# Choosing experts: a second top 16 over 72 sums, a 16-bit key lookup, and another share of weight splits between two engines

## The chip, the core and the metric

The kernel runs on one core of one Trainium2 chip. The metric is the device time of one execution, in microseconds (us). The engines are TensorE (PE in the profile, with its weight loads as PEld), VectorE (DVE), ScalarE (ACT), GpSimd (POOL) and SyncE (SP, which issues the weight loads from memory here).

## What is computed

The reference is a network of two blocks over 256 tokens of 1024 features: a block with two mixers and a layer of 16,384 experts, and two layers of a second kind. Only the experts' layer matters here. Each of 8 heads forms two queries of 128 features for a token and scores them against 128 sub keys each. The 16 best of either side give 256 sums, the 16 best sums name 16 experts, and their scores become softmax weights.

```python
def peer(h, w_pq, sub_keys, expert_u, expert_v):
    ...
        q = (xb @ w_pq).reshape(PEER_BLOCK, PEER_HEADS, 2, PEER_DKH)
        s = jnp.einsum('thpd,hpkd->thpk', q, sub_keys).astype(jnp.float32)
        sv, si = lax.top_k(s, PEER_TOPK)
        cand = (sv[:, :, 0, :, None] + sv[:, :, 1, None, :]).reshape(PEER_BLOCK, PEER_HEADS, -1)
        cidx = (si[:, :, 0, :, None] * N_KEYS + si[:, :, 1, None, :]).reshape(PEER_BLOCK, PEER_HEADS, -1)
        best, pos = lax.top_k(cand, PEER_TOPK)
        eidx = jnp.take_along_axis(cidx, pos, axis=-1)
        g = jax.nn.softmax(best, axis=-1)
        act = jax.nn.gelu(jnp.einsum('thkd,td->thk', expert_u[eidx], xb).astype(jnp.float32), approximate=False)
        return jnp.einsum('thk,thkd->td', (g * act).astype(xb.dtype), expert_v[eidx])
```

## The kernel before

The kernel does not gather experts. It computes the first product for all 16,384 of them on PE (`A = gelu(U x)`), multiplies in the weight with which a token picked an expert (0 for the rest), and multiplies by V. Products keep full precision by three passes (`mm3`, L272 to L274): a weight piece of 128x1024 is loaded (`raw`), its upper part `wh` is made by ACT (L287), its lower part `wl = raw - wh` by DVE or POOL (`split_into`, L291; the argument `lo` names the engine), and PE multiplies upper by upper (L272), lower by upper and upper by lower (L273, L274). One such piece against 256 tokens is a *tile*: 24 matmuls, 3 for each of 8 groups of 128 features.

In `peer` the stage of interest runs two generators in turn (`lanes`, one step of each). `first()` makes the first 36 (`NJ1`) of 128 tiles of U; `up(j, lo)` is one. `second()` makes the choice: for each of 16 pairs of head and side (`hp`) a tile of the query weight `w_pq`, ACT's copy `pq` of the result, matmuls against the sub keys (`skey`), and for each of two token blocks a `top16` over 128 scores: `max`, `max_index`, `match_replace`, `max`, `max_index`, all on DVE. A `yield` in `second()` lets one tile of U follow. The parts `wh` and `wl` of the stage lie in four buffers each (`self.spool = tp, 4`), raw pieces in six.

`choose` is advanced by `second()` with `next(ch)`. For each head and block it makes the 256 sums `cand` (L1034) and their `top16` into `best` and `pos`. After every second head it looks up keys for 64 picks at once (two heads, two blocks, 16 picks): the position is cut into two digits (`dig`, L1043, L1044; `digf`, L1046), each digit is compared with 0 to 15 (`eq`, L1052), the hits are multiplied by the key numbers `sif` (L1056) and reduced over the 16 (`ijw`, L1058). At the end come the softmax and, behind the last tile of U (`issue_after`), six transposes on PE (L1076), whose result `IJ` and `W2` ACT copies. Everything behind waits for them: the next stage builds one-hot rows (`oo`, L939, on DVE; `ow`, L941, on POOL) and goes through the other 92 tiles of U.

Ahead of the stage stands `join`: the end of a norm over the tokens' features, for block 0 and then block 1. Its inverse root is nine operations of one column on DVE (`rsqrt`, L400 to L408, named `rq`), after which ACT makes a diagonal `jdg`, PE transposes, and DVE makes the lower parts of the features.

Each engine works through its instructions in a fixed order, which a scheduling layer has made from the program's order and dependencies. An instruction that waits holds up all behind it on its engine.

Of the kernel before, what the change touches and what calls it, by code (L numbers as in the profile page):

```python
# [38 lines left out]
NE = 1  # L39
LOS = 4  # L40
# [17 lines left out]
# ---------------------------------------------------------------- constants of the shapes  # L58
def consts():
# [71 lines left out]
    # how many of the three dilated windows hold the key, as 8 * log  # L131
# [14 lines left out]
def _fm2(w, cols):  # L146
    """256 columns as two halves of _fm, one behind the other."""
    return np.concatenate([_fm(w, cols[:P]).reshape(P, -1), _fm(w, cols[P:]).reshape(P, -1)], 1)


def _fm(w, cols):
    """[1024, n] columns -> [128, 8, n]: row k*128+p on partition p."""
    w = np.asarray(w)[:, cols]
    return np.ascontiguousarray(w.reshape(-1, P, w.shape[1]).transpose(1, 0, 2))


def _col(v):
    """[m*128] -> [128, m]."""
# [86 lines left out]
class Split:  # L245
    """An operand as the sum of two parts that a float32r pass carries exactly."""
# [11 lines left out]
class Kern:  # L258
# [7 lines left out]
    # ------------------------------------------------------------ small helpers  # L266
# [30 lines left out]
    def raw(self, src, i=0, k=1, n=1024):  # L297
        """Piece i of n columns of src, as k rows."""
# [10 lines left out]
    def wsplit(self, src, n=1024, **kw):  # L309
        """Parts of a piece of a weight that lies in SBUF."""  # L310
# [6 lines left out]
    def wtail(self, src):  # L317
        """Parts of a piece of a weight [P, 1024], each half on its own."""
# [6 lines left out]
    def finish(self, acc, parts):  # L325
        """The last terms of a sum in four banks (token block, half of the features): first those of block 0."""
# [10 lines left out]
    def stack(self, pieces):  # L337
        """Parts of pieces [P, KD, 128] of a weight, side by side."""
# [7 lines left out]
    def stacked(self, ws, hT, b, toks):  # L346
        """Features of a token block, tokens on partitions: steps for the products and for the way out of PSUM."""
# [8 lines left out]
    def rowmm(self, sums, hT, b):  # L356
        """Sums over the features of a token block, tokens on partitions; the lower parts of the features last."""
# [9 lines left out]
    def unstack(self, toks, out):  # L367
        """out[:, i * T + t] = the features i * 128 .. of token t, from both token blocks."""
# [4 lines left out]
    def warm(self, n):  # L373
        """Keeps the clock of the tensor engine up while it has nothing to do."""
# [15 lines left out]
    def cols_of(self, out, r):  # L390
        """The same for rows that lie in SBUF."""
# [4 lines left out]
    def rsqrt(self, a):  # L396
        """1/sqrt of a few columns: a first guess r from the bits, then r * p(a r^2), p in two quadratic factors."""
# [13 lines left out]
    def rsqrt_cols(self, src, n, scale):  # L411
        """1/sqrt(scale * src + EPS)."""
# [4 lines left out]
    def bcast_row(self, out, col, start=True):  # L417
        """out[p, t] = col[t] for 128 tokens."""
# [10 lines left out]
    def S(self, shape, dt=F32, name="t"):  # L429
        """A tile from the slots of its size class; a slot is free again after the last use of its tile."""  # L430
# [13 lines left out]
    # ------------------------------------------------------------ the program  # L444
# [31 lines left out]
    # ------------------------------------------------------------ block 1 up to the experts  # L476
    def block1(self):
# [20 lines left out]
        # norm1: statistics per token  # L498
# [15 lines left out]
        def modulate(c):  # L514
            """Shift and scale of 128 features; the sum over the rows of the weight in two parts."""
# [20 lines left out]
        def feature(c):  # L536
            """128 features of the tokens on partitions: context tokens, then latent ones."""
# [15 lines left out]
        def latents(c):  # L553
            """What these features add to the latents of MLA."""
# [1442 lines left out]
```

## Time and profile before

| | |
|---|---|
| time, median of 3 runs | 1949.08 us (1948.21 to 1951.96) |
| span of the profiled execution | 1946.6 us |
| PE busy | 1861.9 us, 96% |
| DVE busy | 1343.9 us, 69% |
| ACT busy | 970.3 us, 50% |
| POOL busy | 370.0 us, 19% |
| PE's share of the chain that ended last | 80% |
| DVE's share of it | 14% |

The profile is of one execution on the chip, whose time is its span and some 2.5 us around it by the median of the runs. The busy shares are means over stages that differ. The stage in question begins at about 283 us, where PE takes up the tile `hp = 0`, and ends at about 470 us with the transposes of the choice.

### The profile page before, as it was taken

The page shows a single profiled execution, that of the slowest core. Times are in us where ns is not written, and L with a number is a line of the kernel's source. Part 1 is how long each engine was busy: PE and PEld are TensorE (multiplying, and loading weights), DVE is VectorE, ACT ScalarE, POOL GpSimd, SP SyncE. Part 2 cuts the span into 40 slices and gives each one's busy share as a digit, 9 for nine tenths or more (in the row PEclk, how much of TensorE's full clock was granted, in tenths as well). Part 3 has the DMA queues.
Part 4 walks back from the last instruction along what each step waited for, and adds up shares of the span by engine and source line. Part 5 has one row for each costly group of instructions (what it writes and reads, how often), then busy time and mean ns, then how long its engine had stood idle before and what let it go on. Part 6 is the DMA issues. An engine that isn't in the chain of part 4 may idle for free.

```text
span 1946.6 us, 32774 instructions
## 1 busy us (share of the span) xinstructions
PE 1861.9 (96%) x12634; PEld 1653.5 (85%) x12634; DVE 1343.9 (69%) x2820; ACT 970.3 (50%) x1792; POOL 370.0 (19%) x263
## 2 busy tenths in 40 slices
PE   7999988899999999999999999998999999989998
PEld 6775578889999999988888879987999899879997
DVE  4536669988678888655555565577788655767785
ACT  4435443334444444544444556445666564456563
POOL 0000024445554444000000002330100023300000
PEclk9999999899999999999999999999999999999999
DMA  8732544443444444655655672412567334225671
GB/s 307 242 108 87 181 135 138 145 149 125 150 141 141 142 141 143 211 188 187 191 185 184 195 246 92 137 66 87 170 220 239 120 98 131 66 87 163 195 231 62
DMA packets 85101, 302.93 MB, mean 156 GB/s; under 512 B 10096, under 2 KB 10992, under 8 KB 84816
## 3 DMA queue, kind: packets, MB, share of 16 engines
q1 hardware_dynamic: 84944, 300.83, 47.4%
q8 instruction: 99, 1.62, 0.4%
q14 instruction: 58, 0.48, 0.1%
HBM read 298.56 MB, written 2.10 MB: 154 GB/s over the span
## 4 chain that ended last, share of the span: by engine, by line
PE 80%; DVE 14%; ACT 3%; DMA 1%; issue 1%; SPq 0%; POOLq 0%; DVEq 0%; POOL 0%; ACTq 0%
PE b L274 21%; PE b L272 20%; PE b L273 20%; PE b L277 15%; DVE wl L291 3%; DVE eq L1056 1%; DVE oo L939 1%; PE b L1122 1%; PE b L522 1%; DMA raw<-in_wv 1%; PE b L1313 1%; ACT wh L287 1%; DVE eq L1052 0%; DVE cand L1034 0%; ACT jj L722 0%
## 5 line engine op out<-in xcount | busy, mean ns | idle before, releaser
L287 ACT ACTIVATE wh<-raw 128x1024 fp32r<-128x1024 f32 x457 | 483.8, 1061 | 575.0 <-PE b L273 265.2
L291 DVE TENSOR_TENSOR wl<-raw,wh 128x1024 fp32r<-128x1024 f32 x398 | 533.6, 1341 | 264.5 <-ACT wh L287 264.1
L274 PE MATMUL b<-r,wl 128*128 128x256 f32 (+1 forms) x1216 | 350.2, 288 | 26.3 <-DVE wl L291 26.3
L272 PE MATMUL b<-r,wh 128*128 128x256 f32 (+1 forms) x1216 | 353.7, 291 | 0.0
L273 PE MATMUL b<-r,wh 128*128 128x256 f32 x1152 | 325.2, 282 | 0.0
L291 POOL TENSOR_TENSOR wl<-raw,wh 128x1024 fp32r<-128x1024 f32 x59 | 147.2, 2498 | 919.9 <-ACT wh L287 919.8
L272 PE MATMUL b<-hh,wh 128*128 128x256 f32 x1056 | 301.6, 286 | 1.7 <-DVE ast L1638 1.7
L274 PE MATMUL b<-hh,wl 128*128 128x256 f32 x1056 | 299.6, 284 | 1.8 <-DVE wl L291 1.7
L273 PE MATMUL b<-hl,wh 128*128 128x256 f32 x1056 | 298.6, 283 | 0.0
L274 PEld LDWEIGHTS b<-r,wl 128*128 128x128 f32 x1216 | 233.2, 192 | 35.0 <-DVE wl L291 33.4
L272 PEld LDWEIGHTS b<-r,wh 128*128 128x128 f32 x1216 | 234.0, 193 | 3.2 <-issue 1.5
L273 PEld LDWEIGHTS b<-r,wh 128*128 128x128 f32 x1152 | 220.9, 192 | 0.0
L272 PEld LDWEIGHTS b<-hh,wh 128*128 128x128 f32 x1056 | 202.2, 192 | 4.4 <-DVE ast L1638 2.2
L274 PEld LDWEIGHTS b<-hh,wl 128*128 128x128 f32 x1056 | 202.2, 191 | 3.1 <-DVE wl L291 3.0
L273 PEld LDWEIGHTS b<-hl,wh 128*128 128x128 f32 x1056 | 202.3, 192 | 1.4
L273 PE MATMUL b<-wl,k 128*128 128x512 f32 x492 | 194.9, 396 | 1.2 <-DVE wl L291 1.2
L272 PE MATMUL b<-wh,k 128*128 128x512 f32 x492 | 194.7, 396 | 0.0
L274 PE MATMUL b<-wh,k 128*128 128x512 f32 x492 | 194.6, 396 | 0.0
L941 POOL TENSOR_TENSOR ow<-oo,W 128x512 f16<-128x512 f16 x128 | 152.1, 1209 | 161.4 <-DVE oo L939 78.6
L1945 POOL TENSOR_TENSOR u<-u 128x256 f32<-128x256 f32 x44 | 33.5, 762 | 460.0 <-DVE u L1942 297.9
L273 PEld LDWEIGHTS b<-wl,k 128*128 128x128 f32 x492 | 92.4, 188 | 24.7 <-DVE wl L291 2.5
L274 PEld LDWEIGHTS b<-wh,k 128*128 128x128 f32 x492 | 92.4, 188 | 22.3
(480 smaller groups left out, 3189.6 us busy)
## 6 DMA issues: line engine op xcount, KB each, us to landing
raw<-in_eu SPq DMA_DIRECT2D x128, 512.0 KB, 3.9
raw<-in_ev SPq DMA_DIRECT2D x128, 512.0 KB, 3.5
raw<-in_fi SPq DMA_DIRECT2D x88, 512.0 KB, 4.6
raw<-in_w_ada SPq DMA_DIRECT2D x48, 512.0 KB, 5.5
raw<-in_wi SPq DMA_DIRECT2D x48, 512.0 KB, 3.9
raw<-in_fo SPq DMA_DIRECT2D x44, 512.0 KB, 4.6
raw<-in_w SPq DMA_DIRECT2D x16, 512.0 KB, 6.8
raw<-in_w_pq SPq DMA_DIRECT2D x16, 512.0 KB, 4.2
```

The lines of the kernel that those rows point to most:

```text
L272: mm(out, L.hi, R.hi, start=start, stop=False, skip_group_check=True)
L273: mm(out, L.hi, R.lo, start=False, stop=False, skip_group_check=True)
L274: self.lastmm = mm(out, L.lo, R.hi, start=False, stop=stop, skip_group_check=True)
L277: self.nc.tensor.matmul(out, l, r, start=start, stop=stop, skip_group_check=True)
L287: nc.scalar.activation(dst.hi, src, AF.Copy)
L291: e.tensor_tensor(dst.lo, src, dst.hi.bitcast(F32), op=OP.subtract)
L522: nc.tensor.matmul(pa[32 * j:32 * j + 32, :P], self.s2[:, 4 * h + k], wa[:, k, m * P:(m + 1) * P], start=(k == 0), stop=(k == 3), tile_pos ...
L939: nc.vector.tensor_tensor(oo[:, i], iota, IJ[:, i, None, ts].to_broadcast(B), op=OP.is_equal)
L941: nc.gpsimd.tensor_tensor(ow[:, h], oo[:, 1], W2[:, h, None, ts].to_broadcast(B), op=OP.mult)
L1056: nc.vector.tensor_tensor(e4, e4, sif[:, i, p, :, None, :].to_broadcast([P, 2, TOPK, TOPK]), op=OP.mult)
L1122: nc.tensor.matmul(pa[32 * j:32 * j + 32], self.s2[:, k], wa[:, j % 2 * 512:(j % 2 + 1) * 512], start=(k == 0), stop=(k == KD - 1), tile_p ...
L1945: nc.gpsimd.tensor_tensor(u[:, 0], u[:, 0], u[:, 1], op=OP.mult)
```

## The change

Four things change in `peer` and `choose`; a few comments and texts fall away, which shifts line numbers.

- The second top 16 looks at 72 of the 256 sums. With both lists of 16 in falling order, the sum of place a and place b can be among the 16 best only if (a + 1)(b + 1) is at most 16. Four rectangles cover these pairs: a of 0 to 1 with 16 places b, 2 to 3 with 8, 4 to 7 with 4, 8 to 15 with 1. `SV` and `SI` are laid out anew, so that both token blocks of a head are summed by one operation for each rectangle.
- The position in the 72 is turned into (a, b) by a chain of small operations on 64 columns. The lookup works on 16-bit numbers: one comparison and one multiply over 2 x 16 x 64 columns, three halving sums, and four small sums into `ijw`.
- A lookup is now two steps of `choose` (positions, then lookup), and `second()` has a `yield` ahead of every `next(ch)`, so that one tile of U stands between any two steps.
- POOL makes the lower part `wl` of 4 tiles of the query weight (`POOLQ`) and 15 of U (`POOLU`): 19 of the stage's 51, where it made 35. DVE makes the others.

```diff
+POOLQ = 3, 7, 11, 15
+POOLU = 2, 4, 6, 9, 11, 13, 16, 18, 20, 23, 25, 27, 30, 32, 34
...
-                pa = up(j, "dve" if j % 4 == 3 else "pool")
+                pa = up(j, "pool" if j in POOLU else "dve")
...
-        SV = tp.tile([P, 16, 2, TOPK], F32, name="SV")
-        SI = tp.tile([P, 16, 2, TOPK], U32, name="SI")
+        SV = tp.tile([P, 2, 2 * PH, TOPK], F32, name="SV")
+        SI = tp.tile([P, 2, 2 * PH, TOPK], U32, name="SI")
...
-                    w = self.wsplit(self.raw(I["w_pq"][hp // 2], hp % 2, KD), lo="pool" if hp % 2 else "dve")
+                    w = self.wsplit(self.raw(I["w_pq"][hp // 2], hp % 2, KD), lo="pool" if hp in POOLQ else "dve")
...
                 if hp % 2:
+                    yield
+                    next(ch)
+                if hp % 4 == 3:
+                    yield
                     next(ch)
                     yield
-                if hp % 4 == 3:
                     next(ch)
-                    yield
             next(ch)
...
+        io32 = tp.tile([P, TOPK, n], F16, name="io32")
...
+        nc.vector.tensor_copy(io32, io16[:, :, None].to_broadcast([P, TOPK, n]))
...
+        for a0, a1, w in ((0, 2, 16), (2, 4, 8), (4, 8, 4), (8, 16, 1)):
+            stairs.append((a0, a1, w, o))
+            o += (a1 - a0) * w
...
         for h in range(PH):
+            cand = tp.tile([P, 2, o], F32, tag="cand", name="cand", bufs=2)
+            hb = slice(2 * h, 2 * h + 2)
+            for a0, a1, w, at in stairs:
+                B = [P, 2, a1 - a0, w]
+                v.tensor_tensor(cand[:, :, at:at + (a1 - a0) * w].rearrange("p b (a c) -> p b a c", c=w),
+                                SV[:, 0, hb, a0:a1, None].to_broadcast(B),
+                                SV[:, 1, hb, None, 0:w].to_broadcast(B), op=OP.add)
             for b in range(2):
-                B = [P, TOPK, TOPK]
-                cand = tp.tile(B, F32, tag="cand", name="cand", bufs=2)
-                nc.vector.tensor_tensor(cand, SV[:, 2 * h, b, :, None].to_broadcast(B),
-                                        SV[:, 2 * h + 1, b, None, :].to_broadcast(B), op=OP.add)
-                self.top16(tp, cand.rearrange("p a b -> p (a b)"), best[:, h, b], pos[:, h, b])
+                self.top16(tp, cand[:, b], best[:, 2 * h + b], pos[:, 2 * h + b])
             yield
...
-            for p in range(2):
-                B = [P, n, TOPK]
-                eq = tp.tile(B, F32, tag="eq", name="eq", bufs=2)
-                nc.vector.tensor_tensor(eq, digf[:, p, :, None].to_broadcast(B),
-                                        io16[:, None, :].to_broadcast(B), op=OP.is_equal)
...
+            v.tensor_copy(p0.rearrange("p (k g) -> p g k", g=4), pos[:, hs])
+            sh = T2("sh", U32, 3)
+            for i, by in enumerate((4, 3, 2)):
+                v.tensor_scalar(sh[:, i], p0, by, None, op0=OP.logical_shift_right)
+            t, ab = T2("t", F32, 4), T2("ab", F16, 2)
+            v.scalar_tensor_tensor(t[:, 0], sh[:, 1], -2.0, sh[:, 0], op0=OP.add, op1=OP.max)
+            v.scalar_tensor_tensor(t[:, 1], sh[:, 2], -8.0, t[:, 0], op0=OP.add, op1=OP.max)
+            v.scalar_tensor_tensor(t[:, 0], p0, -56.0, t[:, 1], op0=OP.add, op1=OP.max)
...
+            eq = tp.tile([P, 2, TOPK, n], F16, tag="eq", name="eq", bufs=1)
+            B = [P, 2, TOPK, n]
+            v.tensor_tensor(eq, ab[:, :, None, :].to_broadcast(B), io32[:, None].to_broadcast(B), op=OP.is_equal)
+            e4 = eq.rearrange("p q c (k g) -> p (q c) k g", g=4)
+            v.tensor_tensor(e4, e4, sif[:, :, None, :].to_broadcast([P, 2 * TOPK, TOPK, 4]), op=OP.mult)
+            for m in (8, 4, 2):
+                v.tensor_tensor(eq[:, :, 0:m], eq[:, :, 0:m], eq[:, :, m:2 * m], op=OP.add)
+            for q in range(2):
+                e2 = eq[:, q, 0:2].rearrange("p c (k h b) -> p c k h b", h=2, b=2)
+                for b in range(2):
+                    v.tensor_tensor(ijw[:, q, b, h - 1:h + 1].rearrange("p h k -> p k h"), e2[:, 0, :, :, b],
+                                    e2[:, 1, :, :, b], op=OP.add)
+            yield
```

The order on DVE at the end of the norm ahead of the stage, before (`rq` are the nine small operations, `h` and `r` belong to the features of block 0, `iota` serves the next stage):

```order
L400 TENSOR_SCALAR rq<-jtt 128x1
L780 TENSOR_SCALAR h_2559<-b,a_2423,mod_1601 128x128
L401 TENSOR_SCALAR rq<-rq 128x1
L850 CAST iota<-io_2620 128x512
L402 TENSOR_TENSOR rq<-rq 128x1
L403 TENSOR_SCALAR rq<-rq 128x1
L781 TENSOR_TENSOR r<-h_2559,r 128x128
L404 TENSOR_TENSOR rq<-rq,jtt 128x1
L405 SCALAR_TENSOR_TENSOR rq<-rq 128x1
```

The same place after the change, from the fourth of the small operations:

```order
L405 TENSOR_SCALAR rq<-rq 128x1
L783 TENSOR_TENSOR r<-h_2559,r 128x128
L406 TENSOR_TENSOR rq<-rq,jtt 128x1
L293 TENSOR_TENSOR wl<-raw,wh 128x1024
L407 SCALAR_TENSOR_TENSOR rq<-rq 128x1
L408 SCALAR_TENSOR_TENSOR rq<-rq 128x1
L293 TENSOR_TENSOR wl<-raw,wh 128x1024
L409 SCALAR_TENSOR_TENSOR rq<-rq 128x1
L293 TENSOR_TENSOR wl<-raw,wh 128x1024
L410 SCALAR_TENSOR_TENSOR rq<-rq 128x1
L1036 CAST io_2821<-io_2822 128x1024
```

Three splits that were POOL's, and the copy that makes `io32`, now stand in DVE's queue between and behind the small operations.

The order on DVE at the first lookup (heads 0 and 1), before:

```order
L1043 TENSOR_SCALAR dig<-pos 128x64
L1044 TENSOR_SCALAR dig<-pos 128x64
L1046 CAST digf<-dig 128x128
L1052 TENSOR_TENSOR eq<-digf,io_2789 128x1024 x2
L1056 TENSOR_TENSOR eq<-eq,sif 128x512 x3
L1058 TENSOR_REDUCE ijw<-eq 128x2x2x16
L1056 TENSOR_TENSOR eq<-eq,sif 128x512
L1015 MAX SV<-b 128x8
L1058 TENSOR_REDUCE ijw<-eq 128x2x2x16
```

The same place after, from the last of the small operations on 64 columns:

```order
L1077 TENSOR_TENSOR t<-t 128x64
L1078 SCALAR_TENSOR_TENSOR ab<-p_3086,t 128x64
L1085 TENSOR_TENSOR eq<-ab,io_2821 128x2048
L1087 TENSOR_TENSOR eq<-eq,sif 128x2048
L293 TENSOR_TENSOR wl<-raw,wh 128x1024
L1089 TENSOR_TENSOR eq<-eq 128x2x512
L1089 TENSOR_TENSOR eq<-eq 128x2x256
L1089 TENSOR_TENSOR eq<-eq 128x2x128
L1020 MAX SV<-b 128x8
L1093 TENSOR_TENSOR ijw<-eq 128x16x2 x4
```

The reductions are gone, sums of two operands stand in their place, and a split has come between the parts of the lookup.

The order on DVE at the end of the stage, before (`ex` and `sm` belong to the softmax; the last two splits are the next stage's):

```order
L1058 TENSOR_REDUCE ijw<-eq 128x2x2x16
L1069 RECIPROCAL rc<-sm 128x16
L291 TENSOR_TENSOR wl<-raw,wh 128x1024
L1071 TENSOR_TENSOR ijw<-ex,rc 128x128 x2
L291 TENSOR_TENSOR wl<-raw,wh 128x1024 x2
```

After:

```order
L1089 TENSOR_TENSOR eq<-eq 128x2x512
L293 TENSOR_TENSOR wl<-raw,wh 128x1024
L1089 TENSOR_TENSOR eq<-eq 128x2x256
L1089 TENSOR_TENSOR eq<-eq 128x2x128
L1093 TENSOR_TENSOR ijw<-eq 128x16x2 x4
L944 TENSOR_TENSOR oo<-iota,IJ 128x512 x2
```

The next stage's two splits now come ahead of the last `ijw` (one is shown, the other stands a lookup earlier), and nothing but the next stage's `oo` behind it.

## Rows read from the trace of the kernel before

**Rows 1.** The page: span of the profiled execution.
```profile
span 1946.6 us, 32774 instructions
```
**Rows 2.** Busy time by stretch: us, each engine's busy us (instructions), PEclk, DMA share, GB/s.
```profile
280.00:472.00 192.00, 168.69 (x1347) 167.88 (x1348) 170.60 (x491) 75.28 (x119) 80.56 (x32) 0.91 0.42 137
300.00:320.00 20.00, 20.00 (x173) 20.00 (x172) 18.21 (x67) 9.17 (x14) 11.91 (x5) 1.00 0.47 153
342.00:344.00 2.00, 2.00 (x11) 2.00 (x11) 2.00 (x9) 0.94 (x1) 0.00 (x0) 0.50 0.29 117
```
**Rows 3.** Waits, 284 to 472 us: who for whom, us in total, times, longest.
```profile
PE b L274 <- DVE wl L291: 23.3, 4, 8.0
...
DVE SV L1015 <- PE b L277: 11.8, 7, 3.8
```
**Rows 4.** Timeline, PE: start, us, instruction, count [idle before, releaser].
```profile
338.17 0.58 PE L274 MATMUL b<-r,wl 128*128 128x256 f32 x1 [6.89 <-DVE wl L291]
...
464.52 0.58 PE L274 MATMUL b<-r,wl 128*128 128x256 f32 x1 [3.62 <-DVE wl L291]
...
469.38 1.36 PE L1076 MATMUL b<-ident,ijw 128*128 128x128 f32 x6
```
**Rows 5.** Groups by shape, 284 to 472 us: count, busy us, mean ns, idle before.
```profile
L291 POOL TENSOR_TENSOR wl<-raw,wh 128x1024 fp32r<-128x1024 f32 x31 | 79.8, 2580 | 98.5 <-ACT wh L287 98.5
...
L1056 DVE TENSOR_TENSOR eq<-eq,sif 128x512 f32<-128x512 f32 x16 | 28.7, 1834 | 0.0
L291 DVE TENSOR_TENSOR wl<-raw,wh 128x1024 fp32r<-128x1024 f32 x18 | 23.7, 1320 | 0.8 <-ACT wh L287 0.8
L1034 DVE TENSOR_TENSOR cand<-SV 128x256 f32<-128x256 f32 x16 | 15.4, 964 | 0.0
...
L1043 DVE TENSOR_SCALAR dig<-pos 128x64 uint32<-128x64 uint32 x4 | 4.7, 1171 | 0.1
```
**Rows 6.** Timeline, DVE: passes over 256 columns, then over 128.
```profile
302.34 0.40 DVE L1015 MAX8 best<-cand 128x8 f32<-128x256 f32 x1
302.67 0.07 DVE L1019 MATCH_VALUE_LOAD pos<-best,tm 128x8 f32 x1
...
305.69 0.29 DVE L1015 MAX8 SV<-b 128x8 f32<-128x128 f32 x1
305.89 0.28 DVE L1018 MAX8 SV<-tm 128x8 f32<-128x128 f32 x1
```
**Rows 7.** Timeline, DVE: a lookup while POOL does nothing.
```profile
405.78 0.19 DVE L1044 TENSOR_SCALAR dig<-pos 128x64 uint32<-128x64 uint32 x1
406.00 0.23 DVE L1046 CAST digf<-dig 128x128 f32<-128x128 uint32 x1
406.26 2.36 DVE L1052 TENSOR_TENSOR eq<-digf,io 128x1024 f32<-128x1024 f32 x2
408.54 1.89 DVE L1056 TENSOR_TENSOR eq<-eq,sif 128x512 f32<-128x512 f32 x3
410.35 1.21 DVE L1058 TENSOR_REDUCE ijw<-eq 128x64 f32<-128x1024 f32 x1
```
**Rows 8.** Timeline, DVE: end of the norm ahead of the stage.
```profile
271.81 2.00 DVE L781 TENSOR_TENSOR r<-h,r 128x128 fp32r<-128x128 f32 x1
...
274.17 2.12 DVE L850 CAST iota<-io 128x512 f16<-128x512 f32 x1
276.21 2.29 DVE L402 TENSOR_TENSOR rq<-rq 128x1 f32<-128x1 f32 x1
```
**Rows 9.** Timeline, POOL: the same place.
```profile
270.90 7.58 POOL L291 TENSOR_TENSOR wl<-raw,wh 128x1024 fp32r<-128x1024 f32 x3 [3.13 <-ACT wh L287]
```
**Rows 10.** Timeline, DVE: end of the stage.
```profile
462.12 2.35 DVE L291 TENSOR_TENSOR wl<-raw,wh 128x1024 fp32r<-128x1024 f32 x2
```
**Rows 11.** By tile: the next stage's 16-bit comparison, ns min/median/max, first and last start.
```profile
L939 DVE TENSOR_TENSOR oo<-iota,IJ x128: 406/415/1280, 470.7 to 767.8; 128x512 f16<-128x512 f16 x128
```
**Rows 12.** Timeline, DVE: the last lookup's multiplies; POOL splits until 456.8 us.
```profile
448.80 8.57 DVE L1056 TENSOR_TENSOR eq<-eq,sif 128x512 f32<-128x512 f32 x3
```

More of the change, by code (lines that the diff above doesn't have):

```diff
@@ L1047, in choose @@
-            sif = tp.tile([P, 2, 2, 2, TOPK], F32, tag="sif", name="sif", bufs=2)
-            nc.vector.tensor_copy(sif.rearrange("p h q b k -> p (h q) b k"), SI[:, 2 * h - 2:2 * h + 2])
-            for p in range(2):
-                B = [P, n, TOPK]
-                eq = tp.tile(B, F32, tag="eq", name="eq", bufs=2)
-                nc.vector.tensor_tensor(eq, digf[:, p, :, None].to_broadcast(B),
-                                        io16[:, None, :].to_broadcast(B), op=OP.is_equal)
-                for i in range(2):
-                    e4 = eq[:, 32 * i:32 * i + 32].rearrange("p (b k) c -> p b k c", b=2)
-                    nc.vector.tensor_tensor(e4, e4, sif[:, i, p, :, None, :].to_broadcast([P, 2, TOPK, TOPK]),
-                                            op=OP.mult)
-                nc.vector.tensor_reduce(ijw[:, p, :, hs].rearrange("p b h k -> p h b k"),
-                                        eq.rearrange("p (h b k) c -> p h b k c", h=2, b=2), axis=AX.X, op=OP.add)
@@ new lines, in choose @@
+            v.scalar_tensor_tensor(t[:, 1], sh[:, 2], -8.0, t[:, 0], op0=OP.add, op1=OP.max)
+            v.scalar_tensor_tensor(t[:, 0], p0, -56.0, t[:, 1], op0=OP.add, op1=OP.max)
+            a = t[:, 0]
+            v.tensor_copy(ab[:, 0], a)
+            v.tensor_scalar(t[:, 1], a, 8.0, 16.0, op0=OP.mult, op1=OP.add)
+            v.scalar_tensor_tensor(t[:, 1], a, 16.0, t[:, 1], op0=OP.mult, op1=OP.min)
+            v.tensor_scalar(t[:, 2], a, 4.0, 32.0, op0=OP.mult, op1=OP.add)
+            v.scalar_tensor_tensor(t[:, 2], a, 56.0, t[:, 2], op0=OP.add, op1=OP.min)
@@ new lines, in choose @@
+            v.tensor_tensor(t[:, 3], t[:, 1], t[:, 2], op=OP.min)
+            v.scalar_tensor_tensor(ab[:, 1], p0, 0.0, t[:, 3], op0=OP.add, op1=OP.subtract)
+            sif = tp.tile([P, 2 * TOPK, 4], F16, tag="sif", name="sif", bufs=2)
+            v.tensor_copy(sif.rearrange("p (q c) g -> p q g c", q=2), SI[:, :, hs])
+            yield
+            eq = tp.tile([P, 2, TOPK, n], F16, tag="eq", name="eq", bufs=1)
+            B = [P, 2, TOPK, n]
+            v.tensor_tensor(eq, ab[:, :, None, :].to_broadcast(B), io32[:, None].to_broadcast(B), op=OP.is_equal)
@@ L1063, in choose @@
+            yield
+        B = [P, 2 * PH, TOPK]
         e = tp.tile(B, F32, name="ex")
-        nc.vector.tensor_tensor(e, best, best[:, :, :, 0:1].to_broadcast(B), op=OP.subtract)
+        nc.vector.tensor_tensor(e, best, best[:, :, 0:1].to_broadcast(B), op=OP.subtract)
         nc.scalar.activation(e, e, AF.Exp)
-        sm = tp.tile([P, PH, 2], F32, name="sm")
+        sm = tp.tile([P, 2 * PH], F32, name="sm")
         nc.vector.tensor_reduce(sm, e, axis=AX.X, op=OP.add)
-        rc = tp.tile([P, PH, 2], F32, name="rc")
+        rc = tp.tile([P, 2 * PH], F32, name="rc")
```

24 lines of the change are left out of this document (12 added, 12 removed).

## Prediction

> **What bounds the kernel now.** I read the page first, for the span of 1946.6 us [rows 1]; the median of the three runs, 1949.1 us, lies 2.5 us above it, and I carry these 2.5 us along unchanged. The change touches one stage, the choice of experts, so the next view is the busy time of the engines in that stretch [rows 2]. From 280 to 472 us PE ran 1,347 matmuls. In a stretch without waits it runs 173 in 20 us, one in 0.1156 us, so 1,347 are worth 155.7 us: the stage loses 36.3 of its 192 us. DVE is busy for 170.6 of them, more than PE at full speed would need.
>
> The waits say where the 36.3 us go [rows 3]: PE stood still for 23.3 us, in four waits, each for a lower part `wl` that DVE makes. The rest, 13 us, is the clock. [...] The last wait ends at 464.5 us, a tile at the low clock follows, and the six transposes that hand the choice to the next stage run from 469.4 us [rows 4]. Between waits DVE itself waits little: 11.8 us for scores, in seven waits [rows 3]. So DVE sets the pace here, and PE pays for it.
>
> Why is DVE so long? Group its instructions by shape [rows 5]. The multiplies of the lookup take 1834 ns on average, though an undisturbed one takes 0.60 us from start to start [rows 7]. The sums `cand` take 964 ns against 0.40 for another pass over 256 columns [rows 6]. A shift of 64 columns takes 1171 ns against 0.2. All these stretched operations run while POOL makes a `wl` of its own. The clearest case is a one-column operation of 2.29 us in the middle of a POOL run [rows 8, 9]. Added up: multiplies 28.7 - 16 x 0.68 = 17.8 us, sums 15.4 - 16 x 0.41 = 8.8, splits on DVE 23.7 - 18 x 1.2 = 2.1, shifts 4.7 - 4 x 0.2 = 3.9. That is 33 us of DVE being held by 31 POOL splits, 1.05 us for each.
>
> **The change part by part**, on DVE's queue, which is the path.
>
> *Second top 16 over 72 sums.* Five passes over the sums for each of 16 pairs of head and token block, 80 in all. A pass over 256 columns costs 0.33 us from start to start and one over 128 costs 0.20 [rows 6], so 0.13 for 128 columns; 72 columns come to 0.14, an estimate on that line. Saved: 80 x 0.19 = 15.2 us. If short passes stop getting shorter, at 0.20, it is 10.4.
>
> *Making the sums.* Before 16 x 0.33 = 5.3 us. Now four operations a head over 64, 32, 32 and 16 columns, on the same line 0.14 + 0.10 + 0.10 + 0.09 = 0.43 us, times 8 = 3.4. Saved 1.9.
>
> *Lookup, four times (two heads each).* Before, clean: two comparisons 2.28, four multiplies 4 x 0.60, two reductions 2 x 1.13 [rows 7], digits 0.6 and a copy 0.2: 7.7 us. Now: 14 operations over 64 columns at about 0.22, the pace of the digits [rows 7], are 3.1; the copy 0.2; then 16-bit operations. The 16-bit comparison of the next stage takes 0.406 us for 512 columns [rows 11], where 32-bit takes 0.68, so I take half the time per column: 2048 columns 1.14 (twice), then 0.6, 0.33 and 0.2, and four small sums of 0.1. Together 7.1 us. Saved 4 x 0.6 = 2.4. The bound above: at the 32-bit pace per column the 16-bit part is 6.9, not 3.8, which is 12.4 us over four lookups.
>
> *Fewer splits on POOL.* POOL makes 19 of the stage's 51 parts and no longer 35; DVE makes 32 and no longer 16. Three of the new ones stand ahead of the stage (below); 13 lie in it, at 1.14 us for 1024 columns [rows 7]: +14.8 us. Against that, of POOL's 19 one falls ahead of the stage and 18 in it: at 1.05 us of hold each, 18.9 us and no longer 33. Saved 14.1. Bounds: nothing held at all saves 33; the worst is a rival below.
>
> What a split on POOL can hold depends on what DVE has in its queue. The multiplies were stretched, with two operands from SBUF; the reductions, 1.21 us, never were [rows 5, 7]. [...]
>
> *Ahead of the stage.* DVE's order puts three splits and a copy of 1024 columns around the nine small operations of the last norm, for which PE waits. The splits cost 3 x 1.14 = 3.4 us there. But three of POOL's four early splits go: a difference of 2.00, a copy of 2.12 and the one-column operation of 2.29 [rows 8] held by them were to take about 0.3, 0.6 and 0.2, so 5.3 us come back, less 1.05 for the one POOL split that stays. Net -0.8; between +2.2 (the one split holds DVE for its whole length, 2.4 or more, and a split is held too) and -1.9. The copy stands behind the norm's last operation, where DVE waits for PE's transposes, so I cost it at nothing; without that cover 1.1.
>
> *Interleaving.* Between two of the choice's steps there is now always a weight tile, eight tiles of U to four of the query weight where there were seven. Nothing is added; it spreads the lookup so that a split stands between its halves. The four-deep buffers hold four tiles, 4 x 24 x 0.1156 = 11 us of PE work, while a lookup with its split is some 8 us. The weight loads on SP's queue move with the tiles; the stage moved 137 GB/s and an undisturbed stretch 153 [rows 2], so a stage a tenth shorter asks for no rate that it did not already get. ACT, at 75 of 192 us, has room.
>
> *The end.* Before, the last lookup operation is over when the two splits of the next stage start, at 462.1 us [rows 10]. Now these two stand ahead of the last `ijw`: +2.3.
>
> **The sum.** DVE's queue in the stage: -15.2 - 1.9 - 2.4 + 14.8 - 14.1 = -18.8 us; ahead of it -0.8; at the end +2.3. The last `ijw` comes at 462.1 - 17.3 = 444.8. DVE and PE are then nearly equally loaded (PE without waits would need until about 435), and two queues that feed each other lose something: I add two waits of DVE's mean 11.8 / 7 = 1.7 us, 3.4. So 448.2, and the next stage starts 1.1 us later (469.38 to 470.49 before), at 449.3 and not at 470.5: 21.2 us earlier. PE reaches this point after a wait, where before its slow tile was already behind it; at 0.73 us lost in each 2 us [rows 2] some 5 us at the low clock cost about 2. Gain 19. Nothing behind the stage is changed, so 1946.6 - 19 + 2.5 = **1930 us**.
>
> **The rivals.**
>
> 1. *PE becomes the bound.* If holds nearly vanish, all four waits go with their slow tiles: 36.3 us less 1.5 that belong to the slow start ahead of the stage. Time 1914. For it: DVE's clean work falls below PE's 155.7. Against: 18 POOL splits still run among two-input operations. 0.10.
>
> 2. *The holds shrink less than the POOL splits.* What POOL holds is two-input operations and copies, and their share of DVE's work grows. Before: multiplies 9.6, comparisons 9.1, sums 5.3, splits 18, digits and copies 3, of some 137 us (170.6 - 33), a third. Now: small operations 12.4, 16-bit lookup 15.2, sums 3.4, splits 33, copies 1, of about 133, near a half. At 1.5 times the hold, 1.56 us for each of 18, 28 us stay, 9 more than I take: 1939. For it: the reductions at 1.21 us were never stretched [rows 7], and sums of two inputs take their place. Against: passes of the top 16, never stretched either, stay the largest part, and a split that falls wholly among them holds nothing. 0.17. [...]
>
> 3. *Slower.* Each POOL split catches a two-input operation at its start and holds DVE for its whole length. This did happen: three multiplies took 8.57 us [rows 12], 2.86 each, 2.26 lost each. The place is the lookup, now a run of some 25 such operations. At 2.26 x 18 = 40.7 us it is 21.8 more than I take, and 1952; at POOL's whole 2.88 in such a run it would be 1963. It decides from 2.1 us for each split; the mean now is 1.05. 0.06.
>
> 4. *The 16-bit operations run at the 32-bit pace* (operands that repeat, steps of four columns): +12.4, so 1942. Against: the next stage's comparison, at 0.406 us, has the same pattern. 0.05.
>
> 5. *It doesn't do what it says:* the splits that DVE takes over and the dense lookup make PE wait as long as before at other tiles. 1949, 0.07.
>
> **How the numbers follow.** Forecast 0.55; the rivals as given. The range takes in the PE-bound time at the lower end and the two cases of 1939 and 1942 at the upper: 1914 to 1942. A measurement of this kernel tells about 0.2%, 3.9 us, from no change. Faster by more: 0.55 + 0.10 + 0.17 + 0.05 = 0.87; within: 0.07; slower: 0.06.
>
> **What would show it.** In the profile after: passes over 72 columns near 0.23 us long; 16-bit operations over 2048 columns near 1.2; PE's waits for `wl` well under 23 us in total and PEclk at 1.00 more often; the transposes near 448 us; the next stage of the same length. Wrong if the 16-bit operations last over 2 us, if mean durations of DVE's splits rise towards 2 us (rival 2 or 3), or if PE's new wait at the transposes is over 10 us.

## The result, and the profile after

The changed kernel takes 1927.7 us (median of four runs, 1924.75 to 1928.68), the kernel before 1949.0 beside it: a ratio of 0.9885, with a 95% interval of 0.9871 to 0.9900. It is 21.3 us faster; the prediction was 1930 us, in a range of 1914 to 1942. In the changed kernel most lines stand two to five further down: the splits are L293, the three products L274 to L276, transposes and score products L279, the passes of the top 16 L1020 to L1024, the lookup L1062 to L1093, the transposes of the choice L1112.

The page, the busy times by stretch, and the waits from 284 to 455 us (who for whom, us in total, times, longest), to be held against [rows 1 to 3]:

```profile
span 1926.9 us, 32835 instructions
```
```profile
280.00:450.00 170.00, 160.79 (x1340) 159.57 (x1339) 151.69 (x567) 74.15 (x117) 45.85 (x19) 0.98 0.48 157
...
400.00:420.00 20.00, 16.25 (x126) 16.05 (x126) 19.79 (x70) 6.66 (x10) 5.68 (x3) 0.91 0.39 123
```
```profile
PE b L276 <- DVE wl L293: 9.2, 6, 3.8
DVE SV L1020 <- PE b L279: 8.0, 4, 4.9
```

PE waits for `wl` 9.2 us instead of 23.3, and the mean clock of the stage is 0.98, where it was 0.91. What is left of the old picture shows in one stretch: from 400 to 420 us PE runs 126 matmuls and not 173, and its clock falls to 0.91 of full speed, while DVE is busy throughout.

The timeline of PE at three places (start, us, instruction, count, idle before): the transposes of the last norm ahead of the stage, the longest wait in it, and the transposes of the choice that end it, which were at 469.38 us [rows 4].

```profile
277.96 3.78 PE L279 MATMUL b<-jdg,x 128*128 128x128 f32 x16 [7.28 <-ACT jdg L759]
...
411.32 0.38 PE L276 MATMUL b<-r,wl 128*128 128x256 f32 x1 [3.75 <-DVE wl L293]
...
447.92 0.82 PE L1112 MATMUL b<-ident,ijw 128*128 128x128 f32 x6
```

DVE's groups by shape from 284 to 452 us (count, busy us, mean ns, idle before), which answer to [rows 5, 6]:

```profile
L293 DVE TENSOR_TENSOR wl<-raw,wh 128x1024 fp32r<-128x1024 f32 x31 | 46.6, 1502 | 5.5 <-ACT wh L289 5.5
...
L1087 DVE TENSOR_TENSOR eq<-eq,sif 128x2048 f16<-128x2048 f16 x4 | 4.9, 1220 | 0.1
L1085 DVE TENSOR_TENSOR eq<-ab,io 128x2048 f16<-128x2048 f16 x4 | 4.9, 1214 | 0.1
...
L1089 DVE TENSOR_TENSOR eq<-eq 128x512 f16<-128x512 f16 x4 | 3.8, 945 | 0.1
...
L1021 DVE FIND_INDEX8 pos<-best,cand 128x8 uint32<-128x72 f32 x16 | 3.6, 225 | 0.0
...
L1080 DVE CAST sif<-SI 128x128 f16<-128x128 uint32 x4 | 3.4, 856 | 0.0
```

A pass over 72 sums takes 0.225 us, a 16-bit operation over 2048 columns 1.21 to 1.22: both as worked out. The splits at 1502 ns, the sums over 512 columns at 945 and the cast `sif` at 856 are still being held by POOL: in the kernel without POOL below the three take 1212, 410 and 306 ns.

A measure for all that follows is the **stage**: from the start of the norm's transposes (`b<-jdg,x`) to the start of the transposes of the choice (`b<-ident,ijw`). Before it is 469.38 - 279.90 = 189.5 us ([rows 4] and the line below, of the kernel before), after 447.92 - 277.96 = 170.0. PE's own work in it takes 155.8 us at full clock, as the last kernel of the experiments shows. (The 155.7 us of the prediction belong to a slightly longer stretch.)

```profile
279.90 3.39 PE L277 MATMUL b<-jdg,x 128*128 128x128 f32 x16 [7.59 <-ACT jdg L757]
```

### The profile page after: what moved, and what is told of

Read it like the earlier page. It is cut to its first block, busy times and chain, and to the rows that moved or that the text cites. A ratio compares the mean times of both kernels' runs of the same rounds, so it can differ in the third digit from the quotient of the medians.

```text
span 1926.9 us, 32835 instructions
## 1 busy us (share of the span) xinstructions
PE 1857.6 (96%) x12634; PEld 1648.3 (86%) x12634; DVE 1323.7 (69%) x2901; ACT 970.3 (50%) x1792; POOL 328.4 (17%) x247
## 4 chain that ended last, share of the span: by engine, by line
PE 78%; DVE 15%; ACT 3%; DMA 2%; issue 2%; SPq 0%; POOLq 0%; DVEq 0%; POOL 0%; ACTq 0%
PE b L276 20%; PE b L274 20%; PE b L275 20%; PE b L279 15%; DVE wl L293 4%; DVE oo L944 1%; PE b L1158 1%; ACT wh L289 1%; DMA raw<-in_wv 1%; PE b L524 1%; PE b L1349 1%; DVE eq L1089 0%; DVE tm L1022 0%; DVE u L1978 0%; DVE jt L741 0%
## 5 line engine op out<-in xcount | busy, mean ns | idle before, releaser
L293 DVE TENSOR_TENSOR wl<-raw,wh 128x1024 fp32r<-128x1024 f32 x414 | 559.7, 1352 | 270.8 <-ACT wh L289 270.5
L276 PE MATMUL b<-r,wl 128*128 128x256 f32 (+1 forms) x1216 | 347.5, 286 | 12.4 <-DVE wl L293 12.4
L274 PE MATMUL b<-r,wh 128*128 128x256 f32 (+1 forms) x1216 | 351.1, 289 | 0.0
L274 PE MATMUL b<-hh,wh 128*128 128x256 f32 x1056 | 301.6, 286 | 1.8 <-DVE ast L1674 1.8
L276 PE MATMUL b<-hh,wl 128*128 128x256 f32 x1056 | 299.7, 284 | 1.8 <-DVE wl L293 1.7
L293 POOL TENSOR_TENSOR wl<-raw,wh 128x1024 fp32r<-128x1024 f32 x43 | 105.4, 2452 | 941.0 <-ACT wh L289 668.9
L276 PEld LDWEIGHTS b<-r,wl 128*128 128x128 f32 x1216 | 230.1, 189 | 21.3 <-DVE wl L293 19.8
L274 PEld LDWEIGHTS b<-r,wh 128*128 128x128 f32 x1216 | 231.2, 190 | 3.2 <-issue 1.5
L275 PEld LDWEIGHTS b<-r,wh 128*128 128x128 f32 x1152 | 218.3, 189 | 0.0
L274 PEld LDWEIGHTS b<-hh,wh 128*128 128x128 f32 x1056 | 202.2, 192 | 4.5 <-DVE ast L1674 2.3
L276 PEld LDWEIGHTS b<-hh,wl 128*128 128x128 f32 x1056 | 202.2, 191 | 3.1 <-DVE wl L293 3.0
L274 PE MATMUL b<-wh,k 128*128 128x512 f32 x492 | 194.8, 396 | 0.0
L276 PE MATMUL b<-wh,k 128*128 128x512 f32 x492 | 194.6, 395 | 0.0
L274 PEld LDWEIGHTS b<-wh,k 128*128 128x128 f32 x492 | 92.4, 188 | 22.6 <-ACT wh L289 0.4
```

The lines of the kernel that those rows point to most:

```text
L274: mm(out, L.hi, R.hi, start=start, stop=False, skip_group_check=True)
L275: mm(out, L.hi, R.lo, start=False, stop=False, skip_group_check=True)
L276: self.lastmm = mm(out, L.lo, R.hi, start=False, stop=stop, skip_group_check=True)
L293: e.tensor_tensor(dst.lo, src, dst.hi.bitcast(F32), op=OP.subtract)
```

## The experiments

Theory: DVE's queue sets the stage, POOL's splits hold it, and each of the four parts of the change is worth its term. The rivals of the prediction ask how large the holds are and whether PE or DVE is the bound. Most kernels are the changed one with one edit. Two begin with the kernel before, and four with the changed kernel without POOL.

### One part undone: wide passes

```diff
+        cands = [tp.tile([P, 2, 256], F32, name=f"cand{i}") for i in range(2)]
+        for cand in cands:
+            v.memset(cand, -3.0e38)
...
-            cand = tp.tile([P, 2, o], F32, tag="cand", name="cand", bufs=2)
+            cand = cands[h % 2]
```

> The changed kernel, with the second top 16 running over 256 columns again: the 72 sums lie at the front, the other 184 columns are filled once with a very small number. Only the width of the 80 passes is undone. Theory (DVE's queue sets the stage, and a term of it is worth its own length): 80 x 0.19 = 15.2 us come back, PE's waits for wl rise from 9.2 us towards 20 and its clock falls after them: 1927.7 + 15 to 18 = 1943 to 1946. Rival (PE is the bound by now, DVE has room): only what exceeds the room comes back, under 8 us: 1928 to 1935.

1937.96 us, 0.9939 (0.9918 to 0.9960): 10.3 us above the changed kernel, between the two expectations. Groups of DVE, and PE's wait:

```profile
L1021 DVE FIND_INDEX8 pos<-best,cand 128x8 uint32<-128x256 f32 x16 | 6.6, 414 | 0.0
```
```profile
PE b L276 <- DVE wl L293: 16.5, 5, 5.3
```

A pass takes 414 ns and not 225, so 80 of them are 80 x 0.189 = 15.1 us of queue: the term of 15.2 is right as work. The stage grows by 10.4 (457.15 - 276.80 = 180.4). The rest disappears in waits that DVE has anyway: for scores and upper parts it waits 13.5 us from 284 us on in the changed kernel and 7.7 here.

### One part undone: a 32-bit lookup

```diff
-        io32 = tp.tile([P, TOPK, n], F16, name="io32")
+        io32 = tp.tile([P, TOPK, n], F32, name="io32")
...
-            t, ab = T2("t", F32, 4), T2("ab", F16, 2)
+            t, ab = T2("t", F32, 4), T2("ab", F32, 2)
```

(`sif` and `eq` likewise.)

> The changed kernel with the lookup's four tiles (io32, ab, sif, eq) in 32 bits. Theory: each of the four lookups is longer by 6.9 - 3.8 = 3.1 us, 12.4 in all, and DVE's queue passes them on: 1938 to 1942. The comparison over 2048 columns takes 2.2 us and not 1.2. Rival (the lookup stands where PE has four finished tiles in hand, so its length is covered): under 5 us, 1928 to 1933.

1939.55 us, 0.9957 (0.9940 to 0.9973), 11.9 more. Groups of DVE, and PE at both ends of the stage:

```profile
L1089 DVE TENSOR_TENSOR eq<-eq 128x1024 f32<-128x1024 f32 x4 | 9.3, 2324 | 0.0
L1087 DVE TENSOR_TENSOR eq<-eq,sif 128x2048 f32<-128x2048 f32 x4 | 9.1, 2287 | 0.1
```
```profile
271.36 3.34 PE L279 MATMUL b<-jdg,x 128*128 128x128 f32 x16 [2.28 <-ACT jdg L759]
```
```profile
456.82 0.82 PE L1112 MATMUL b<-ident,ijw 128*128 128x128 f32 x6
```

The total meets the 12.4 of the theory. The stage is 185.5 us, 15.5 more, but not all of this is the lookup. In this kernel the scheduling layer put no split between the norm's small operations. So 6.6 us came back ahead of the stage, and three of DVE's splits, 3 x 1.14 = 3.4 us, lie inside it that stood ahead of it in the changed kernel. Without them some 12 us are left. The halving sum over 1024 columns lasts as long as the product over 2048 beside it (2324 and 2287 ns), where the last of the four takes 1.22 us (at 450.19 us); so it is held for some 1.1 us on average. Wide operations of two inputs are among what POOL catches.

### The share of POOL, in both kernels

The changed kernel with the old share, and the kernel before with the new share:

```diff
-                pa = up(j, "pool" if j in POOLU else "dve")
+                pa = up(j, "dve" if j % 4 == 3 else "pool")
```

> The changed kernel with POOL making the old share of lower parts (odd hp; every j except each fourth: 35 of 51, not 19). Theory, by one hold of 1.05 us for each POOL split: DVE's own splits fall by 13 x 1.14 = 14.8 us in the stage, holds rise by 13 x 1.05 = 13.7, ahead of the stage 0.8 comes back: 1927 to 1930, within the noise of the changed kernel. Rival (the new order exposes more two-input operations, the hold is 1.5 us and more for each split): 13 x 1.5 = 19.5 against 14.8, and PE's waits grow: 1932 to 1938. Other rival (POOL's split takes 2.4 us and PE comes to wait for POOL): waits of PE for POOL in the list, 1935 or more.

> The kernel before with the new share of lower parts alone (POOLQ and POOLU: 19 of 51 on POOL): the old 256 sums, lookup and steps stay. Theory, with the holds as measured since (1.2 to 1.4 us a split where two-input work is dense, 1.1 in the kernel before): DVE's queue gets 13 x 1.14 = 14.8 us more of splits and 14 to 18 us fewer holds in the stage, about 1 us comes back ahead of it: 1944 to 1949, no change that can be told. Rival (the share is where the change's gain lies): 1935 or less. Other rival (splits on DVE queue up behind the long lookups): 1953 or more.

The old share in the changed kernel: 1930.25 us, 0.9901 (0.9881 to 0.9922), 2.5 us slower, which the spread of the runs hardly tells from nothing. The place of the norm's transposes (280.43) accounts for all of it; its stage is 169.3, as long as with the new share. Against the means of the kernel without POOL below, its 31 POOL splits hold DVE for some 37 us, 1.20 each, nearer to the theory's 1.05 than to the rival's 1.5. The new share in the kernel before: 1954.4 us, 1.0024 (1.0013 to 1.0036), slower, and PE waits longer:

```profile
PE b L276 <- DVE wl L293: 30.6, 5, 8.5
```

The theory, no change, fell there, and the second rival's time came. Its reason, splits that queue up behind long lookups, is argued and not shown: DVE's own waits for the upper parts that ACT makes grew too, from 0.8 to 15.4 us. So the share alone is worth nothing inside the stage of the changed kernel, and costs 5 us in the old one.

### No POOL at all, in both kernels

```diff
-POOLQ = 3, 7, 11, 15
-POOLU = 2, 4, 6, 9, 11, 13, 16, 18, 20, 23, 25, 27, 30, 32, 34
+POOLQ = ()
+POOLU = ()
```

> The changed kernel with all 51 lower parts of the stage made by DVE, none by POOL. Theory: DVE's splits rise by 18 x 1.14 = 20.5 us in the stage, the holds (18 x 1.05 = 18.9 us) go, so DVE's queue is the same within 2 us: 1926 to 1933, and no operation of DVE in the stage is stretched: the sums of 32 columns at 0.15 us and not 0.24, the copy sif at 0.2 and not 0.86. Rival (holds cost less than they seem, since DVE would have waited anyway): 1940 to 1948.

> The kernel before with all lower parts of the stage on DVE, nothing else changed. Theory A (a split on POOL costs DVE its hold, one on DVE its own 1.14 us): 31 x 1.14 = 35.3 us more against some 36 us of holds gone, 2 us back ahead of the stage: 1944 to 1949. Theory B (without POOL more goes than the holds, as the kernel without POOL was 10 us faster than by holds alone: parts that come late from POOL keep buffers and with them ACT and DVE waiting): 1933 to 1940. The multiplies of the lookup are at 0.68 us each in either case.

The changed kernel: **1911.9 us**, 0.9809 (0.9789 to 0.9829). Neither expectation reaches so low. The kernel before: 1946.2 us, 0.9980 (0.9971 to 0.9990); its stage is 466.26 - 276.82 = 189.4 us, unchanged, and its gain lies ahead of the stage, as theory A has it:

```profile
276.82 3.78 PE L277 MATMUL b<-jdg,x 128*128 128x128 f32 x16 [5.13 <-ACT jdg L757]
...
466.26 0.82 PE L1076 MATMUL b<-ident,ijw 128*128 128x128 f32 x6
```

In the changed kernel without POOL, the busy times, PE's only wait, DVE's splits, and PE at both ends of the stage:

```profile
300.00:320.00 20.00, 20.00 (x174) 20.00 (x173) 18.06 (x76) 9.32 (x14) 0.00 (x0) 1.00 0.54 181
...
400.00:420.00 20.00, 20.00 (x173) 20.00 (x173) 18.73 (x90) 10.54 (x15) 0.00 (x0) 1.00 0.60 197
```
```profile
PE b L276 <- DVE wl L293: 0.8, 1, 0.8
```
```profile
L293 DVE TENSOR_TENSOR wl<-raw,wh 128x1024 fp32r<-128x1024 f32 x49 | 59.4, 1212 | 0.4 <-ACT wh L289 0.4
```
```profile
275.87 3.68 PE L279 MATMUL b<-jdg,x 128*128 128x128 f32 x16 [5.13 <-ACT jdg L759]
...
432.67 0.97 PE L1112 MATMUL b<-ident,ijw 128*128 128x128 f32 x6
```

The stage is 432.67 - 275.87 = 156.8 us, 1.0 more than PE's own work. Its 49 splits take 1212 ns each (284 to 434 us). Set against the means of this kernel, the changed kernel's groups are held for 24.7 us: splits 9.0, `ijw` 2.2, sums over 512 and 256 columns 2.1 and 2.2, shifts 2.1, `cand` 3.0, casts 4.3 (rounded parts). That is 1.37 us for each of 18 POOL splits on average, and a split of DVE's own costs 1.14. From DVE's first pass to its last `ijw` the queue shrinks from 157.9 to 147.2 us: busy time from 146.9 to 140.4, DVE's idle time from 11.0 to 6.9. Only 24.7 - 18 x 1.14 = 4.2 us of this are the difference of the two prices. The other 2.3 us of busy time have no cause shown; the idle time belongs to the next question. With 140 us of work DVE stays below PE's 155.8, and PE's waits and its low clock are gone together: one wait of 0.8 us, and a clock of 1.00 in every 20 us from 280 to 440 us.

### Is it the hold, or that POOL is late?

POOL's splits also come late and keep buffers. Two tests. First, six buffers where there were four:

```diff
-        self.spool = tp, 4
+        self.spool = tp, 6
```

> The changed kernel with six buffers in place of four for the parts of the stage's weight tiles, so that a part that POOL makes late keeps no buffer from ACT and DVE; shares, order of the choice and holds are those of the changed kernel. Rival to the theory of the hold (the 16 us between the changed kernel and the one without POOL come in good part from the buffers): below 1921. Theory (hold): 1924 to 1929, since DVE's queue is as long as before and only waits of DVE and ACT for each other (5.5 us in the trace) can shrink; PE's four waits of 9.2 us for DVE's parts can shrink to some 5.

1922.1 us, 0.9856 (0.9837 to 0.9876), 5.6 below the changed kernel and between the expectations. The profiled run is the longest of its four, 1925.95 us. PE at both ends of the stage, and then a wait inside it, of ACT and of PE (timelines):

```profile
273.75 3.52 PE L279 MATMUL b<-jdg,x 128*128 128x128 f32 x16 [2.28 <-ACT jdg L759]
```
```profile
444.33 0.82 PE L1112 MATMUL b<-ident,ijw 128*128 128x128 f32 x6
```
```profile
417.08 1.06 ACT L289 ACTIVATE wh<-raw 128x1024 fp32r<-128x1024 f32 x1 [9.44 <-DMA raw<-in_eu]
```
```profile
421.47 1.22 PE L279 MATMUL b<-skey,pq 128*128 128x128 f32 x4 [9.12 <-ACT pq L885]
```

In this run the stage is 170.6 us, not shorter; 4.2 us come from the norm ahead of it. Inside, DVE finishes its last `ijw` at 437.8, 8.6 us earlier. From its first pass its queue is 150.5 us and no longer 157.9, and its idle time 4.6 and no longer 11.0. So the four buffers do cost DVE time; that parts which come late keep them is the likely reason, though not shown by itself. PE gains nothing by the six, because it loses 9.1 us in one new wait for ACT's `pq`; ahead of that ACT waited 9.4 us for a weight load. What the buffers give where no load comes late is not shown.

Second, the kernel without POOL, and 18 POOL instructions that nobody waits for, on a buffer of their own:

```diff
+        def hold():
+            with self.tc.issue_after(self.lastwh.ins):
+                nc.gpsimd.tensor_tensor(held[:, 1], held[:, 0], held[:, 0], op=OP.subtract)
...
+                if j in HOLDU:
+                    hold()
```

> The kernel with all 51 splits of the stage on DVE (1911.9 us), to which 18 subtractions of 128x1024 on POOL are added. They read and write a buffer of their own, nobody waits for them, each may start only when ACT has made the upper part of the tile at which POOL worked in the changed kernel. So POOL is busy as before, but no weight part comes late and no buffer is kept. Theory (POOL's reading holds DVE, 1.37 us each by the changed kernel's durations): 24.7 us more in DVE's queue, of which 3 to 6 go into DVE's own waits: 1930 to 1937, the transposes at 451 to 458 us, one-column or short two-input operations stretched again. Rival A (the parts that POOL hands over late, and the buffers that they keep, were the cost, not the hold): below 1918. Rival B (half and half): 1918 to 1929.

> The same 18 idle instructions as copies of 128x1024, one input instead of two. Theory (a reading POOL instruction holds for its whole length, whatever its number of inputs): as the subtractions if the copy is as long, in proportion if it is shorter: 1920 to 1937 for lengths of 1.2 to 2.5 us. Rival (only a two-input POOL instruction holds): 1909 to 1916.

> The same 18 idle instructions of POOL, but as fills of 128x1024 with a constant: they write and read nothing. [...] Rival (any access of POOL holds DVE): the fill holds as the subtraction does, per us of its length; at half the length or more of a subtraction that is 12 us or more, above 1921.

In the traces the 18 did not keep to their tiles: they ran one behind the other, the subtractions and copies at the start of the stage, the fills well ahead of it. (POOL's timeline of the three kernels:)

```profile
279.74 46.44 POOL L864 TENSOR_TENSOR held<-held 128x1024 f32<-128x1024 f32 x18 [279.30 <-ACT pq L897]
```
```profile
280.28 29.94 POOL L864 COPY held<-held 128x1024 f32<-128x1024 f32 x18 [279.84 <-ACT pq L897]
```
```profile
232.39 18.13 POOL L864 MEMSET held<- 128x1024 f32 x18 [231.94 <-ACT PT L1366]
```

*Subtractions:* 1927.9 us, 0.9893 (0.9873 to 0.9913), 16.0 us above the kernel without POOL and as slow as the changed one. DVE's groups in these 46 us, and PE at both ends of the stage:

```profile
L294 DVE TENSOR_TENSOR wl<-raw,wh 128x1024 fp32r<-128x1024 f32 x12 | 23.6, 1981 | 0.0
L1063 DVE TENSOR_TENSOR cand<-SV 128x32 f32<-128x32 f32 x4 | 3.6, 928 | 0.0
L1063 DVE TENSOR_TENSOR cand<-SV 128x16 f32<-128x16 f32 x2 | 3.5, 1725 | 0.0
...
L1033 DVE FIND_INDEX8 SI<-SV,b 128x8 uint32<-128x128 f32 x8 | 2.3, 288 | 0.0
```
```profile
272.53 3.62 PE L280 MATMUL b<-jdg,x 128*128 128x128 f32 x16 [2.28 <-ACT jdg L760]
...
446.88 0.97 PE L1124 MATMUL b<-ident,ijw 128*128 128x128 f32 x6 [1.57 <-DVE ijw L1105]
```

Against the clean means that is 9.2 us on twelve splits, 9.0 on the sums and 1.5 on a copy: 19.7, or 1.09 for each subtraction, and the stage grows by 17.6 (446.88 - 272.53 = 174.4). Passes of the top 16 stay at 288 ns. Nobody waits for POOL here, so POOL's work alone, with no part that comes late, holds DVE, and the hold costs time. That the 16 us are also the distance between the changed kernel and the one without POOL is chance: there the hold replaces splits of DVE's own, and the two prices differ by 4.2 us in all. My 24.7 us were too much for this place, where DVE's queue is mostly passes: 1930 to 1937 was missed by 2 us, in the band of rival B, though not for its reason.

*Copies:* 1914.5 us, 0.9817 (0.9796 to 0.9838), 2.6 us. The theory's 1920 was missed; the rival's number holds but not its reason, since splits are still stretched, to 1541 ns for 11 of them (1212 without POOL). In all some 6.3 us are held, 0.35 for each copy of 1.66 us: per us of POOL's time half of what a subtraction holds. What makes the difference stays open. In this kernel and in the one with subtractions no split stands among the norm's small operations, as in the last kernel below (1908.8 us), which is therefore the nearer one to compare. Above it the subtractions cost 19.1 us and the copies 5.7, close to the 19.7 and 6.3 us that they hold.

*Fills:* 1914.4 us, 0.9817 (0.9799 to 0.9836). They ran in another stage, so the time tells nothing of this one; what they overlapped with does (DVE's timeline):

```profile
242.27 0.17 DVE L417 TENSOR_SCALAR rqa<-b 128x8 f32<-128x8 f32 x1 [0.92 <-PE b L280]
242.47 1.00 DVE L403 TENSOR_SCALAR rq<-rqa 128x8 uint32<-128x8 uint32 x1
243.51 0.97 DVE L404 TENSOR_SCALAR rq<-rq 128x8 uint32<-128x8 uint32 x1
244.52 0.17 DVE L405 TENSOR_TENSOR rq<-rq 128x8 f32<-128x8 f32 x1
...
248.80 1.22 DVE L294 TENSOR_TENSOR wl<-raw,wh 128x1024 fp32r<-128x1024 f32 x1
```

Six splits under the fills took 1.22 us each, as without them, and a product of two operands 0.17; three one-input operations of 8 columns took 0.89 to 1.00, about a whole fill (0.95), where they take 0.17 without. A fourth, `rqa`, which reads PE's result `b`, took its 0.17. (One more product of two inputs shows 0.78 us; it begins 0.12 us behind a held operation and ends with it.) So the rival, by which any access of POOL holds DVE, is right for the three at 0.89 to 1.00 us and wrong for the splits at 1.22. What in the form of the three decides is not shown.

### The interleaving, and the best version

The old order of steps in the changed kernel:

```diff
                 if hp % 2:
-                    yield
                     next(ch)
-                if hp % 4 == 3:
                     yield
-                    next(ch)
+                if hp % 4 == 3:
+                    next(ch)
+                    next(ch)
                     yield
-                    next(ch)
```

> The changed kernel with the old interleaving: no tile of U between the steps of a head pair, so sums, positions and lookup stand in one run (28 tiles of U among the choice's steps, 8 behind, where the change has 32 and 4). Theory: that run is some 14 us of DVE work, more than the 11 us of four finished tiles, so PE waits at each of four lookups some 3 us longer than now and its clock falls behind: 1932 to 1942. Rival (only the length of DVE's whole queue counts, not how it is cut): 1925 to 1930.

1929.3 us, 0.9894 (0.9878 to 0.9911), a stage of 171.2: the interleaving is worth 1.2 to 1.6 us, which the spread of the runs does not tell from nothing. The rival's range holds, by which only the total of the queue counts.

The kernel without POOL still puts splits between the norm's small operations. Holding these and the copy `io32` back (the tile `hp = 1` likewise):

```diff
+            with self.tc.issue_after(root.ins) if j < 3 else ExitStack():
+                w = self.wsplit(self.raw(I["eu"][j // 2], j % 2), lo=lo).r("p (k c) -> p k c", k=KD)
...
+        with self.tc.issue_after(self.root.ins):
+            nc.vector.tensor_copy(io32, io16[:, :, None].to_broadcast([P, TOPK, n]))
```

> The kernel without POOL in the stage, and with the first four lower parts and the copy io32 ordered behind the last of the nine small operations of the norm ahead of the stage. Theory: the norm ends 3 x 1.14 = 3.4 us earlier, PE's wait for the diagonal falls from about 5 to under 2 us, the four parts still come before PE needs them: 1911.9 - 3.4 = 1908, up to 1.5 us less if PE's clock stays up through its transposes. Rival (the parts now come too late for the first tiles): PE waits for wl at the first tiles by as much, 1911 to 1914.

**1908.8 us**, 0.9786 (0.9770 to 0.9803), as forecast, the fastest of all. PE at both ends:

```profile
272.16 2.05 PE L279 MATMUL b<-jdg,x 128*128 128x128 f32 x16 [2.11 <-ACT jdg L759]
```
```profile
428.11 0.97 PE L1116 MATMUL b<-ident,ijw 128*128 128x128 f32 x6
```

The stage is 156.0 us, PE is busy for 155.8 of them, and its mean clock is 1.00 (284 to 430 us). PE is the bound of the stage now, and a shorter queue on DVE has nothing more to give there.

## Why the prediction was right, and where it was lucky

**The mechanism held.** DVE's queue set the stage, PE paid by waits and by the clock that followed them, and a shorter queue gave both back. Before, the clock stood at 0.50 of full speed from 342 to 344 us, behind the wait of 6.89 us that ended at 338.17 [rows 2, 4]; after, at 0.50 from 414 to 416 us, behind the one of 3.75 us that ended at 411.32. The times say the same: DVE's first pass came 0.9 us earlier, its queue ended at 446.4 us (forecast 444.8), and the transposes moved by 21.5 us (forecast 21.2).

**Passes.** 0.225 us each, 15.1 us of queue for 15.2 forecast. At the end of the stage they are worth 10.4, as the wide kernel shows: a term of a queue that also waits is not a gain of the same size.

**Lookup.** The 16-bit pace was right (1.21 us long, for 1.14 forecast from start to start), and so was rival 4's price of 12.4: 32 bits cost 11.9.

**Holds, the mis-sized term.** I took 33 us before, 1.05 for each POOL split, and 18.9 after. Before I left two groups out, the second shift and the cast `sif`; with them it is 36 us, 1.16 each. After it is 24.7, 1.37 each. The term gave 11.3 us, not 14.1. Rival 2 named a reason, a larger share of two-input operations and copies in DVE's work, and its price of 1.56 was too high; the truth lies between. The reason is not shown: with the old share the same work of DVE is held for 1.20 by each of 31 POOL splits.

**Share.** The forecast set +14.8 for DVE's new splits against -14.1 for the holds, a wash, and in the stage it was one (170.0 against 169.3 us). What I did not ask is the next question: at 1.37 against 1.14, a split left on POOL is a loss on average. Rival 1 stands for that case at 1914 us, and the kernel without POOL reached 1911.9.

**Ahead of the stage.** Forecast -0.8, with a bound of -1.9; measured -1.9. The one POOL split there still held a one-column operation of the norm, which takes 0.15 us in the kernel without POOL (DVE's and POOL's timelines, [rows 8, 9] before):

```profile
272.69 2.30 DVE L407 SCALAR_TENSOR_TENSOR rq<-rq 128x1 f32<-128x1 f32 x1
```
```profile
272.53 2.45 POOL L293 TENSOR_TENSOR wl<-raw,wh 128x1024 fp32r<-128x1024 f32 x1 [272.09 <-DMA x_wait<-x]
```

**Idle time and clock.** I added 3.4 us of new mutual waits; DVE's idle time from its first pass to the last `ijw` was 10.1 us before and 11.0 after. I added 2 us at the low clock behind the transposes; PE had no wait there, and the granted clock is 1.00 from 449 to 455 us. These two errors cover the mis-sized hold, which is luck.

**Behind the stage.** Of the 21.5 us, 20.3 are left at the norm of the second block and 19.7 at the last product of the run. The chain has weight loads of 3.7 to 6.2 us in it at the end of the product with V, which could be the place of the loss, but runs of either kernel differ by up to 4 us in themselves, so this stays open. The 4 us of idle time that DVE has beside POOL in the changed kernel, and not without it, were gone with six buffers too. So they have to do with the four buffers, as far as one profile tells.

## What to carry to other kernels

Price the help of a second engine by what it does to the first: here a split moved to POOL saved DVE 1.14 us and held it for 1.37 on average, and DVE also waited more, so no help was faster. The whole gain was 16 us; the two prices account for 4.2 of them. When two engines are nearly level, find which of them would be the bound without the other's interference, and aim at that time. And undo each part in turn: one that is neutral or harmful alone (the share, 5 us slower in the old kernel) can hide in a change that is good.

## What the runs showed of the hardware

A POOL instruction held DVE by form, not only by length: 1.09 to 1.37 us for a subtraction of 2.4 to 2.6 us, 0.35 for a copy of 1.66, and under fills of 0.95 us three one-input operations of DVE took 0.89 to 1.00 us, where they take 0.17, while one that reads PE's result (0.17) and the operations with two inputs (1.22 for a split, 0.17 for a product) kept their time, but for one of 0.78 us that began behind a held one. Beside a subtraction a one-column operation with two inputs went from 0.15 to 2.30 us. Passes of the top 16 were stretched neither by subtractions nor by copies (288 ns beside either), and reductions not by subtractions (1.20 us on average, 1.21 for one that ran wholly beside a split of POOL at 374.8 us in the kernel before); no run has them beside fills.
